# Merge stage of a hybrid encoder layer: weights loaded raw and parted on the spot, and no longer parted ahead by GpSimd

## The chip, the cores and the metric

One core of a Trainium2 chip runs the whole layer in one launch. The metric is the device time of the launch in microseconds (us). An engine takes its instructions strictly in the order in which they stand in its queue: PE (TensorE), DVE (VectorE), ACT (ScalarE), POOL (GpSimd) and SP (SyncE, which here only issues transfers). A wait at the head of a queue holds everything behind it.

## The reference

`x` is 1024 positions by 1024 channels. The layer is

```
h      = LayerNorm(x) * (1 + sc1) + sh1            # sh, sc, g: from c through w_ada
q,k,v, f, q,k,v, gate_a, gate_c = split(h @ w_in)
o_a    = forgetting attention, 8 heads             # causal, bias from a cumulated gate
o_c    = chunk attention, 8 heads                  # 64-position chunks, own and 8 before, learned bias
merged = sigmoid(gate_a) * (o_a @ w_br_fox) + sigmoid(gate_c) * (o_c @ w_br_chunk)
x      = LayerNorm(alpha * x + (1 + g1) * (merged @ w_out))
h      = LayerNorm(x) * (1 + sc2) + sh2
x      = LayerNorm(alpha * x + (1 + g2) * (convolved, gated MLP of h))
```

All is float32. A product of two float32 matrices is made of three PE products: each operand is **parted** into a rounded high part and the rest, `hi = round(x)`, `lo = x - hi`, and `hi*hi + hi*lo + lo*hi` is summed.

## The kernel before, in words

The work goes through stages: the first norm and modulation, attention with the projections beside it, the merge stage, the up-projection, the down-projection. A scheduler places the instructions on each engine's queue; the code gives it the program order.

**Attention.** `plan` goes through pairs of heads, the eight chunk heads first (pairs 4 to 7), then the eight forgetting heads. Scores are made by PE (L442, L443), a bias is added and the extreme taken by DVE (L451), the exponential by ACT (L457), PE turns the result (L494), ACT and DVE part it (L497, L498), and PE multiplies by v (L508). A chunk head's bias tile `cb` comes from DRAM, but two 64x64 corners of it are the mask, and these are written by POOL: `load_bias`, L415 and L416. There are eight such pairs of memsets, one for each chunk head, and the first L451 of a head reads its tile. The tile has two buffers; the call for a head comes when the head before it starts.

**Side work.** While attention runs, the generator `side_work` feeds POOL. It is advanced by the attention loop (`next(beside, None)`) and yields twice for each job, so jobs and memsets stand on the POOL queue in the order in which the loop came by. A job is one of three kinds:

- split job, 16 of them: load a 512 KB weight tile of `w_out` or `w_br` (L546), round it (L550, two halves), take the rest (L553, two halves), store both (L595, two stores of 512 KB) into the DRAM tensors `wod` and `brd`;
- combining job, 19 of them: load two weight tiles, make four sums or differences of halves (L588, four instructions), store two tiles into `wd` (8 jobs, from `w_up`) or `td` (11 jobs, from `w_down`);
- vector job, 32 of them: load a tile of `w_ada`, two products with the conditioning (L556) and two sums into `acc` (L559).

They are dealt in groups of seven, "jajaaja": three jobs (j) and four vector jobs (a). The j list holds the 16 split jobs first, then the 8 of `w_up`, then the 11 of `w_down`. Tiles `dr` have four buffers in turn, so a load waits for the stores of the tile four places before it. After the side work POOL loads and scales the first attention outputs (L788, L792, L793).

**Merge stage.** For each half of the positions, `merge` multiplies by the branch weights (eight sets `c`, 24 matmuls each, `psb`) and gates (`sg`, loaded by SP; L928, L934 to L938), and `mix` multiplies by `w_out` (eight sets `k`, 24 matmuls each, `psm`). In the first half both go set by set. In the second half `merge(1)` has the norms of the first half beside it (`norms`: DVE, ACT, and stores `xd` on POOL, L994), two of the `w_out` sets are fetched early into a pool of their own (`widened`, `wide`), and `mix(1)` does set 0 for all four position tiles, then each tile with all the other sets.

A set is fetched by `parted_w` (L907 to L913): two loads of 512 KB from `wod` or `brd` on SP, straight into `wh`, `wl`, or, for every third set, into the two buffers of `ws`. No engine touches it before PE.

Of the kernel before, what the change touches and what calls it, by code (L numbers as in the profile page):

```python
# [12 lines left out]
F32 = mybir.dt.float32  # L13
F32R = mybir.dt.float32r
# [5 lines left out]
P = 128  # L20
S = 1024
D = 1024
NT = S // P
KD = D // P
H = 512
# [19 lines left out]
def body(ctx, tc, a, out):  # L45
# [50 lines left out]
    wod = dram.tile([KD, 4, P, H], F32, name="wod", tag="wod")  # L96
    brd = dram.tile([KD, 4, P, H], F32, name="brd", tag="brd")

    def load_w(src, shape):
        if shape[-1] == P:  # L100
# [414 lines left out]
    def side_work():  # L515
# [1 line left out]


        sub = ALU.subtract
        jobs = [([src.rearrange("p (j n) -> p j n", j=2), None], None, dst)  # L520
                for srcs, dst in ((a["w_out"], wod), (a["w_br"].rearrange("c p k n -> c p (k n)"), brd))
                for src, dst in zip([srcs[k] for k in range(KD)], [dst[k] for k in range(KD)])]
        ups = ((3, 2, 3, ALU.add), (2, 0, 2, sub), (0, 3, 0, sub), (1, 1, 0, sub))
        downs = ((0, 1, 0, sub), (1, 3, 1, sub), (3, 3, 0, sub), (2, 2, 3, sub))
        for c in range(HEAD):
# [16 lines left out]
        def fetch():  # L542
            while len(tiles) < min(len(loads), free[0]):
                x = ap.tile([P, 2, H], F32, name=nm("dr"), tag="dr", bufs=4)
                if loads[len(tiles)] is not None:
                    po.dma_start(out=x, in_=loads[len(tiles)])  # L546
                tiles.append(x)

        def copied(x, y, j):
            po.tensor_copy(out=y[:, j, :].bitcast(F32R), in_=x[:, j, :])  # L550

        def rest(x, y, j):
            po.tensor_sub(out=x[:, j, :].bitcast(F32R), in0=x[:, j, :], in1=y[:, j, :].bitcast(F32R))  # L553

        def product(acc, x, k):
            po.tensor_scalar_mul(x[:, k % 2, :] if k else acc, x[:, k % 2, :], cond[:, k : k + 1])  # L556
# [7 lines left out]
        for m, (srcs, what, dst) in enumerate(mixed):  # L564
            xs = tiles[at : at + len(srcs)]
            while bias:
                bias.pop()()
            if due and m >= due[0][0] + LAG:
                _, acc_, v, half = due.pop(0)
                ps = pmm.tile([P, H], F32, name=nm("psada"), tag="mm")  # L570
                ada_sums(ps, acc_, H)
                bias.append(partial(late_bias, ps, v, half))
            if dst is None:
                v, half, q = what
                if q == 0:
# [6 lines left out]
            elif what is None:  # L582
                ops = [partial(f, *xs, j) for f in (copied, rest) for j in range(2)]
            else:
                blocks = [x[:, j, :] for x in xs for j in range(2)]
                ops = [partial(po.tensor_tensor, out=blocks[o], in0=blocks[p], in1=blocks[q], op=op) for o, p, q, op in what]
            for j, op in enumerate(ops):
                op()  # L588
# [312 lines left out]

    if True:

        sets = count()

        def parted_w(src, pool=None):

            tags = ("wh", "wl") if pool or next(sets) % 3 < 2 else ("ws", "ws")
            parts = [(pool or wp).tile([P, 2, H], F32R, name=nm(g), tag=g) for g in tags]
            for x, j in zip(parts, (2, 0)):  # L910
                sy.dma_start(out=x.bitcast(F32), in_=src[j : j + 2].rearrange("j p n -> p j n"))
            return parts

        def merge(half, os_, beside, ahead=iter(())):
            ms = []
# [2 lines left out]
            def branch(c, b):  # L918
                if c not in held:
                    sg = mx.tile([P, 2, H], F32, name=nm("sgl"), tag="sgl", bufs=2)  # L920
                    sy.dma_start(out=sg, in_=gd[half, 2 * c : 2 * c + 2].rearrange("b p s -> p b s"))
                    held[c] = [x.rearrange("p j (k n) -> p (j k) n", k=4) for x in parted_w(brd[c])], sg
# [21 lines left out]
        def mix(half, ms, beside, wide=None, ended=None, rest=None):  # L944
# [5 lines left out]
            def add(t, k, w):  # L950
                mh, ml = ms[k]
                ts = slice(t * P, (t + 1) * P)
                for n in range(2):
                    pe.matmul(ps[t][n], mh[:, ts], w[0][:, n, :], start=k == 0, stop=False)
                    pe.matmul(ps[t][n], mh[:, ts], w[1][:, n, :], start=False, stop=False)
                    pe.matmul(ps[t][n], ml[:, ts], w[0][:, n, :], start=False, stop=k == end)

            end = 3 if wide else KD - 1
            late = []
            for k in range(1 if wide else KD):  # L960
                w = parted_w(wod[k])
                for t in range(4):
                    add(t, k, w)
                next(beside, None)
            if wide:
                late += [(k, parted_w(wod[k])) for k in (1, 2)]
                late += sorted(wide.items()) + [(k, parted_w(wod[k], rest)) for k in (6, 7)]
            xs = []
            for t in range(4):
                tt = 4 * half + t  # L970
                xx = mx.tile([P, D], F32, name=nm("xr"), tag="xr", bufs=4)
                sy.dma_start(out=xx, in_=a["x"][tt * P : (tt + 1) * P, :])
                xs.append(xx)
# [70 lines left out]
        reading = load_o(1, o1, (4, 6, 2, 0), mx, "xr", 4, mx, "xr")  # L1044
        xs0 = mix(0, m0, chain((None,) * 2, reading))
        x0, x1 = [], []
        wide_cm, widep = opened(name="wide", bufs=2)
        wide = {}

        def widened():  # L1050
            sy.dma_start(out=l1g, in_=a["ln1_g"].partition_broadcast(P))
            sy.dma_start(out=l1b, in_=a["ln1_b"].partition_broadcast(P))
            for _ in range(5):
                yield
            for k in (4, 5):
                wide[k] = parted_w(wod[k], widep)
                yield

        beside = norms(0, xs0, x0)
# [400 lines left out]
```

## Time and profile before

| what | us |
|---|---|
| runs of the kernel before | 1547.07, 1549.76, 1550.41; median 1549.76 |
| span of the profiled execution | 1548.2 |
| PE busy in it | 1502.7 |
| POOL busy in it | 658.2 |
| attention with its projections, about | 95 to 697 |
| first attention output loaded by POOL after the side work | 651.06 |
| `merge(1)`, first to last matmul | 794.7 to 847.7 |

The profile is that of one execution. Its span runs from the first to the last instruction; the median of the runs is 1.6 us above it, which is what lies around the span and between executions. A row of a timeline has the start, the duration, the engine, the line of the kernel and what is written from what; in square brackets stands how long the engine sat idle ahead of it and whom it waited for. A row of groups has the busy time, the mean in nanoseconds, and the idle time before. In a table of stretches each engine has its busy time, then follow PE's granted clock and the share of time in which the DMA engines were busy.

### The profile page before, as it was taken

How to read it: one execution, taken by the hardware profiler on the slowest of the kernel's cores; microseconds unless marked ns; L12 is line 12 of the kernel's file. 1: busy time of each engine (PE TensorE's matmuls, PEld its weight loads, DVE VectorE, ACT ScalarE, POOL GpSimd, SP SyncE). 2: the span in 40 equal slices, each digit the busy share in tenths (PEclk: the TensorE clock that was granted, in tenths of full speed). 3: DMA queues.
4: the chain of work that ended last, by engine and by line, in shares of the span. 5: the costliest groups of instructions: out<-in, count | busy, mean ns of one | idle time of the engine just before them, and what ended most of it. 6: DMA issues, size and time to landing. Idle time of an engine off the chain costs nothing.

```text
span 1548.2 us, 21760 instructions
## 1 busy us (share of the span) xinstructions
PE 1502.7 (97%) x7663; PEld 1264.7 (82%) x7663; DVE 1034.5 (67%) x2038; ACT 709.5 (46%) x1316; POOL 658.2 (43%) x607
## 2 busy tenths in 40 slices
PE   6999999999999999999998999999999999999996
PEld 3788898889889888888886877888888888888885
DVE  6756566566656565554468587777778776845798
ACT  3545555554544454442112165544544554555451
POOL 0039897787878776730000005454455443000000
PEclk9999999999999999999999999999999999999998
DMA  9156666756576578758999575443344322697552
GB/s 366 50 165 215 217 192 198 218 194 216 189 233 220 189 260 299 260 151 292 308 323 347 214 258 190 140 154 132 122 140 147 115 102 104 246 328 255 191 190 75
DMA packets 129756, 317.54 MB, mean 205 GB/s; under 512 B 13024, under 2 KB 21936, under 8 KB 129648
## 3 DMA queue, kind: packets, MB, share of 16 engines
q1 hardware_dynamic: 90208, 197.83, 37.8%
q0 software_dynamic: 25344, 92.02, 17.8%
q10 hardware_dynamic: 14096, 26.31, 4.8%
q8 instruction: 60, 0.98, 0.3%
q14 instruction: 48, 0.39, 0.1%
HBM read 223.47 MB, written 84.25 MB: 199 GB/s over the span
## 4 chain that ended last, share of the span: by engine, by line
PE 72%; POOL 9%; DMA 8%; DVE 7%; issue 2%; ACT 1%; SPq 0%; ACTq 0%; DVEq 0%; POOLq 0%
PE psu L859 25%; PE psd L1277 4%; PE psd L1278 4%; PE psd L1276 4%; PE pso L508 3%; DMA wod<-dr 3%; PE psg L192 3%; PE psg L194 3%; PE psg L193 3%; POOL dr L553 2%; PE pst L494 2%; POOL acc L559 2%; POOL dr L556 2%; PE psq L194 2%; DMA brd<-dr 2%
## 5 line engine op out<-in xcount | busy, mean ns | idle before, releaser
L859 PE MATMUL psu<-hc,wx 128*128 128x512 f32 x792 | 185.7, 389 | 0.1
L859 PEld LDWEIGHTS psu<-hc,wx 128*128 128x128 f32 x792 | 148.6, 188 | 31.3 <-ACT u L1202 0.5
L1125 DVE SCALAR_TENSOR_TENSOR pcv<-u,convp,pcv 128x1024 f32<-128x1024 f32 x88 | 113.1, 1286 | 45.4 <-ACT pcv L1123 44.4
L1266 DVE TENSOR_TENSOR op<-rw,op 128x512 fp32r<-128x512 f32 x146 | 93.4, 687 | 52.8 <-ACT op L1265 52.5
L1265 ACT CAST op<-rw 128x512 fp32r<-128x512 f32 x146 | 85.2, 622 | 85.4 <-PE psd L1278 39.8
L457 ACT ACTIVATE s<-s,mx 128x640 f32<-128x640 f32 (+7 forms) x128 | 94.5, 738 | 58.6 <-DVE mx L451 57.4
L1277 PE MATMUL psd<-op,op 128*128 128x512 f32 x292 | 113.6, 389 | 0.9 <-DVE op L1266 0.9
L1278 PE MATMUL psd<-op,op 128*128 128x512 f32 x292 | 113.6, 389 | 0.0
L1276 PE MATMUL psd<-op,op 128*128 128x512 f32 x292 | 113.1, 389 | 0.0
L497 ACT CAST pt<-pst 128x512 fp32r<-128x512 f32 (+1 forms) x192 | 82.1, 450 | 62.3 <-PE pst L494 60.8
L498 DVE TENSOR_TENSOR pt<-pst,pt 128x512 fp32r<-128x512 f32 (+1 forms) x192 | 96.0, 519 | 17.2 <-ACT pt L497 15.5
L192 PE MATMUL psq<-h1h,wh 128*128 128x512 f32 x256 | 103.8, 407 | 1.7 <-DVE h1h L188 1.3
L192 PE MATMUL psg<-h1h,wh 128*128 128x512 f32 x256 | 103.7, 405 | 0.0
L194 PE MATMUL psq<-h1h,wl 128*128 128x512 f32 x256 | 100.9, 394 | 0.9 <-DVE wl L112 0.9
L194 PE MATMUL psg<-h1h,wl 128*128 128x512 f32 x256 | 100.3, 392 | 0.5 <-DVE wl L112 0.5
L193 PE MATMUL psq<-h1l,wh 128*128 128x512 f32 x256 | 100.8, 394 | 0.0
L193 PE MATMUL psg<-h1l,wh 128*128 128x512 f32 x256 | 100.2, 391 | 0.0
L556 POOL TENSOR_SCALAR dr<-dr,cond 128x512 f32<-128x512 f32 x56 | 89.9, 1607 | 8.1 <-DMA dr<-in_w_ada 7.1
L508 PE MATMUL pso<-pt,vs 128*128 128x256 f32 x608 | 90.4, 288 | 1.3 <-DVE pt L498 1.2
L994 POOL DMA_DIRECT2D xd<-xr x8 | 4.4, 545 | 199.3 <-DVE xr L992 199.3
L508 PEld LDWEIGHTS pso<-pt,vs 128*128 128x128 f32 x608 | 81.1, 191 | 8.7 <-DVE pt L498 2.6
L112 DVE TENSOR_TENSOR wl<-ws,wh 128x1024 fp32r<-128x1024 f32 x38 | 61.2, 1611 | 39.1 <-ACT wh L111 39.1
(286 smaller groups left out, 4001.3 us busy)
## 6 DMA issues: line engine op xcount, KB each, us to landing
ws<-in_w_up SPq DMA_DIRECT2D x34, 512.0 KB, 3.7
dr<-in_w_ada POOLq DMA_DIRECT2D x32, 512.0 KB, 4.8
dr<-in_w_down POOLq DMA_DIRECT2D x22, 512.0 KB, 4.8
td<-dr POOLq DMA_DIRECT2D x22, 512.0 KB, 4.7
rw<-td SPq DMA_DIRECT2D x44, 256.0 KB, 4.5
yd<-y SPq DMA_DIRECT2D x20, 512.0 KB, 2.7
rw<-yd SPq DMA_DIRECT2D x40, 256.0 KB, 4.2
rw<-sd SPq DMA_DIRECT2D x33, 256.0 KB, 4.6
```

Of the source, the lines that this page charges most:

```text
L192: pe.matmul(ps, wh, xh, start=start, stop=False)
L193: pe.matmul(ps, wh, xl, start=False, stop=False)
L194: pe.matmul(ps, wl, xh, start=False, stop=stop)
L457: se.activation(out=st[:, 0:nk], in_=st[:, 0:nk], func=AF.Exp, scale=-1.0, bias=prev, accum_out=sums[:, col : col + 1])
L498: ve.tensor_sub(out=dl, in0=src, in1=dh)
L508: pe.matmul(ps[:, 0:256], vs[:, h % 2, j0 + j, :], pt[j // 4][:, c, j % 4, :], start=j == 0 and c == 0, stop=j == nj - 1 and c == 1)
L556: po.tensor_scalar_mul(x[:, k % 2, :] if k else acc, x[:, k % 2, :], cond[:, k : k + 1])
L859: pe.matmul(ps, w[:, a_, k, :], h[k][b_], start=first, stop=k == 3 and a_ == 1, skip_group_check=on)
L1125: ve.scalar_tensor_tensor(out=ps, in0=u[b][:, 2 - d : S + 2 - d], scalar=cp[:, 2 - d : 3 - d], in1=ps, op0=ALU.mult, op1=ALU.add)
L1276: pe.matmul(ps[t], g[:, 0, ts], d[:, 0], start=start, stop=False, skip_group_check=on)
L1277: pe.matmul(ps[t], g[:, 0, ts], d[:, 1], start=False, stop=False, skip_group_check=on)
L1278: pe.matmul(ps[t], g[:, 1, ts], d[:, 0], start=False, stop=stop, skip_group_check=on)
```

## The change

The split jobs, `wod` and `brd` go. `side_work` starts with the combining jobs. `parted_w` loads a raw 512 KB tile into `ws` (two buffers), lets ACT round it into `wh` (two buffers) and POOL subtract into `wl` (two buffers). The early pool `wide` holds three sets (3, 4, 5) in place of two, and `mix(1)` fetches set 3 there and no longer last.

```
-        jobs = [([src.rearrange("p (j n) -> p j n", j=2), None], None, dst)
-                for srcs, dst in ((a["w_out"], wod), (a["w_br"].rearrange("c p k n -> c p (k n)"), brd))
-                for src, dst in zip([srcs[k] for k in range(KD)], [dst[k] for k in range(KD)])]
+        jobs = []
...
-        sets = count()
-
         def parted_w(src, pool=None):
-
-            tags = ("wh", "wl") if pool or next(sets) % 3 < 2 else ("ws", "ws")
-            parts = [(pool or wp).tile([P, 2, H], F32R, name=nm(g), tag=g) for g in tags]
-            for x, j in zip(parts, (2, 0)):
-                sy.dma_start(out=x.bitcast(F32), in_=src[j : j + 2].rearrange("j p n -> p j n"))
-            return parts
+            st = wp.tile([P, D], F32, name=nm("ws"), tag="ws")
+            sy.dma_start(out=st, in_=src)
+            hi, lo = [(pool or wp).tile([P, 2, H], F32R, name=nm(g), tag=g) for g in ("wh", "wl")]
+            st = st.rearrange("p (j n) -> p j n", j=2)
+            se.copy(out=hi, in_=st)
+            po.tensor_sub(out=lo, in0=st, in1=hi)
+            return hi, lo
...
             if wide:
-                late += [(k, parted_w(wod[k])) for k in (1, 2)]
-                late += sorted(wide.items()) + [(k, parted_w(wod[k], rest)) for k in (6, 7)]
+                late += [(k, parted_w(a["w_out"][k])) for k in (1, 2)] + sorted(wide.items())
+                late += [(k, parted_w(a["w_out"][k], rest)) for k in (6, 7)]
...
-            if wide:
-                late.append((3, parted_w(wod[3])))
...
-        wide_cm, widep = opened(name="wide", bufs=2)
+        wide_cm, widep = opened(name="wide", bufs=3)
...
-            for _ in range(5):
+            for _ in range(4):
                 yield
-            for k in (4, 5):
-                wide[k] = parted_w(wod[k], widep)
+            for k in (3, 4, 5):
+                wide[k] = parted_w(a["w_out"][k], widep)
                 yield
```

In the rows below an instruction's line is that of its own kernel: the changed kernel's L541, L545, L548, L575, L582, L413 are L546, L556, L559, L588, L595, L415 of the kernel before.

The POOL queue just ahead of the mask of the last chunk head, before:

```order
L595 DMA brd<-dr_3661 128x2x512
L595 DMA brd<-dr_3563 128x2x512
L556 TENSOR_SCALAR dr_3662<-dr_3662,cond 128x512
L546 DMA dr_3712<-in_w_ada 128x2x512
L546 DMA dr_3787<-in_w_br 128x1024
L556 TENSOR_SCALAR dr_3662<-dr_3662,cond 128x512
L556 TENSOR_SCALAR dr_3712<-dr_3712,cond 128x512 x2
L415 MEMSET cb_3463 64x64
```

and after:

```order
L575 TENSOR_TENSOR dr_3574<-dr_3574 128x512
L541 DMA dr_3674<-in_w_ada 128x2x512
L575 TENSOR_TENSOR dr_3574<-dr_3672,dr_3574 128x512
L575 TENSOR_TENSOR dr_3672<-dr_3672,dr_3574 128x512
L582 DMA td<-dr_3574 128x2x512
L575 TENSOR_TENSOR dr_3672<-dr_3672 128x512
L545 TENSOR_SCALAR dr_3674<-dr_3674,cond 128x512
L582 DMA td<-dr_3672 128x2x512
L541 DMA dr_3724<-in_w_ada 128x2x512
L545 TENSOR_SCALAR dr_3674<-dr_3674,cond 128x512
L541 DMA dr_3799<-in_w_down 128x1024
L413 MEMSET cb_3474 64x64
```

Counted over the whole queue, what stands ahead of the masks of the last four chunk heads was 7, 10, 12 and 14 split jobs with 8, 12, 15 and 18.5 vector jobs; it is now 6.25, 8.25, 11.25 and 14.25 combining jobs with 7.5, 10.5, 14.5 and 17.5 vector jobs. The masks stand after nearly as many jobs, but after jobs of another kind.

The POOL queue in `merge(1)`, where there were only the four stores `xd` of the norms, is now (`wl` from `ws` and `wh`: the rest of a set; the sets are branch 3, branch 4, `w_out` 3, branch 5, `w_out` 4, branch 6, `w_out` 5, branch 7):

```order
L897 TENSOR_TENSOR wl_8602<-ws_8599,wh_8601 128x1024
L977 DMA xd<-xr_8389 128x1024
L897 TENSOR_TENSOR wl_8662<-ws_8659,wh_8661 128x1024
L897 TENSOR_TENSOR wl_8701<-ws_8698,wh_8700 128x1024
L977 DMA xd<-xr_8391 128x1024
L897 TENSOR_TENSOR wl_8730<-ws_8727,wh_8729 128x1024
L897 TENSOR_TENSOR wl_8769<-ws_8766,wh_8768 128x1024
L977 DMA xd<-xr_8393 128x1024
L897 TENSOR_TENSOR wl_8797<-ws_8794,wh_8796 128x1024
L897 TENSOR_TENSOR wl_8836<-ws_8833,wh_8835 128x1024
L897 TENSOR_TENSOR wl_8864<-ws_8861,wh_8863 128x1024
```

So from branch 5 on, branch sets and early `w_out` sets take turns in the two `ws` buffers. Each raw load on SP stands in the same turn, and waits for the POOL subtraction two sets before it.

More of the change, by code (lines that the diff above doesn't have):

```diff
@@ L95, in body @@
     rowd = dram.tile([2, D], F32, name="rowd", tag="rowd")
-    wod = dram.tile([KD, 4, P, H], F32, name="wod", tag="wod")
-    brd = dram.tile([KD, 4, P, H], F32, name="brd", tag="brd")
     def load_w(src, shape):
@@ L544, in fetch @@
                 x = ap.tile([P, 2, H], F32, name=nm("dr"), tag="dr", bufs=4)
-                if loads[len(tiles)] is not None:
-                    po.dma_start(out=x, in_=loads[len(tiles)])
+                po.dma_start(out=x, in_=loads[len(tiles)])
                 tiles.append(x)
[L549 to L553, printed above, removed]
         def product(acc, x, k):
@@ L581, in side_work @@
                     due.append((m, acc, v, half))
-            elif what is None:
-                ops = [partial(f, *xs, j) for f in (copied, rest) for j in range(2)]
             else:
@@ L921, in branch @@
                     sy.dma_start(out=sg, in_=gd[half, 2 * c : 2 * c + 2].rearrange("b p s -> p b s"))
-                    held[c] = [x.rearrange("p j (k n) -> p (j k) n", k=4) for x in parted_w(brd[c])], sg
+                    held[c] = [x.rearrange("p j (k n) -> p (j k) n", k=4) for x in parted_w(a["w_br"][c].rearrange("p k n -> p (k n)"))], sg
                 (bh, bl), sg = held[c]
@@ L955, in add @@
                     pe.matmul(ps[t][n], mh[:, ts], w[1][:, n, :], start=False, stop=False)
-                    pe.matmul(ps[t][n], ml[:, ts], w[0][:, n, :], start=False, stop=k == end)
-            end = 3 if wide else KD - 1
+                    pe.matmul(ps[t][n], ml[:, ts], w[0][:, n, :], start=False, stop=k == KD - 1)
             late = []
             for k in range(1 if wide else KD):
-                w = parted_w(wod[k])
+                w = parted_w(a["w_out"][k])
                 for t in range(4):
```

## The prediction

> **What bounds the kernel now.** First the page's span and engine rows, then the table of stretches, then the chain of waits and the timelines around its turning points.
>
> ```profile
> span 1548.2 us, 21760 instructions
> PE 1502.7 (97%) x7663; PEld 1264.7 (82%) x7663; DVE 1034.5 (67%) x2038; ACT 709.5 (46%) x1316; POOL 658.2 (43%) x607
> ```
>
> PE is busy for all but 45 us: a change off PE can win only part of those, and can lose without limit by making PE wait. Stretches (PE, PEld, DVE, ACT, POOL, granted clock, DMA share, GB/s):
>
> ```profile
> 300.00:350.00 50.00, 48.33 (x301) 43.25 (x300) 30.99 (x84) 26.89 (x62) 43.64 (x44) 1.00 0.60 200
> 800.00:820.00 20.00, 19.91 (x88) 16.16 (x87) 19.40 (x43) 3.94 (x7) 1.15 (x2) 1.00 0.82 296
> 820.00:840.00 20.00, 14.83 (x64) 11.33 (x62) 18.05 (x45) 3.94 (x8) 1.07 (x2) 0.98 0.99 370
> 840.00:860.00 20.00, 19.57 (x75) 15.91 (x75) 7.42 (x24) 6.97 (x9) 1.08 (x2) 0.85 0.89 319
> ```
>
> In the attention (300 to 350) POOL is the busiest engine beside PE, 43.64 of 50 us before its transfers and waits are counted. In the merge stage (800 to 860) POOL has nothing to do, the DMA engines are full, and PE loses some microseconds. The chain of waits shows where POOL sets PE's time:
>
> ```profile
> 327.74 3.11 POOL dr L556 x2
> 330.85 0.10 POOL cb L415
> 330.97 0.04 DVE s L451
> 333.09 0.76 PE pst L494 x5
> ```
>
> A product of a vector job (L556), then the mask of a chunk head (L415), then the scores on DVE, then a transpose on PE that came late. So the last mask already ends on the critical path. Masks on POOL, and the moments at which DVE used or wanted them:
>
> ```profile
> 250.92 0.16 POOL L415 MEMSET cb<- 64x64 f32 x1
> 291.71 0.17 POOL L415 MEMSET cb<- 64x64 f32 x1
> 330.79 0.14 POOL L415 MEMSET cb<- 64x64 f32 x1
> ```
> ```profile
> 260.45 0.23 DVE L451 CUSTOM_DVE_ANT_0 s<-pss,cb 128x128 f32<-128x128 f32 x1
> 294.62 0.29 DVE L451 CUSTOM_DVE_ANT_0 s<-pss,cb 128x128 f32<-128x128 f32 x1
> 327.65 0.55 DVE L486 MEMSET pt<- 128x256 f32 x2
> 330.97 0.29 DVE L451 CUSTOM_DVE_ANT_0 s<-pss,cb 128x128 f32<-128x128 f32 x1 [2.77 <-POOL cb L415]
> ```
>
> The sixth mask was written 9.5 us ahead of its use (250.92, 260.45), the seventh 2.9 us (291.71, 294.62), the eighth after DVE was free for it at 328.2 (327.65 + 0.55): DVE waited 2.77 us. POOL falls behind during the chunk heads and has no slack left at their end.
>
> **The change, part by part.** *POOL beside the attention.* Fewer jobs, but the 16 light ones went, and they stood first; the heavy ones move ahead of the masks. The price of both kinds in place, waits included:
>
> ```profile
> 98.86 1.17 POOL L550 CAST dr<-dr 128x512 fp32r<-128x512 f32 x2 [2.86 <-issue]
> 303.38 0.73 POOL L550 CAST dr<-dr 128x512 fp32r<-128x512 f32 x1
> 369.88 1.30 POOL L588 TENSOR_TENSOR dr<-dr 128x512 f32<-128x512 f32 x1 [2.09 <-DMA dr<-in_w_up]
> 491.67 1.52 POOL L588 TENSOR_TENSOR dr<-dr 128x512 f32<-128x512 f32 x1 [2.11 <-DMA dr<-in_w_up]
> ```
> ```profile
> L556 POOL TENSOR_SCALAR dr<-dr,cond 128x512 f32<-128x512 f32 x56 | 89.9, 1607 | 8.1 <-DMA dr<-in_w_ada 7.1
> L559 POOL TENSOR_TENSOR acc<-acc,dr 128x512 f32<-128x512 f32 x56 | 75.3, 1345 | 1.7
> L546 POOL DMA_DIRECT2D dr<-in_w_ada x31 | 23.8, 766 | 33.6 <-DMA brd<-dr 13.4 <-DMA wod<-dr 12.2 <-DMA wd<-dr 6.7
> ```
>
> From the first rounding of split job 1 to that of job 13 there are four groups of three split and four vector jobs: (303.38 - 98.86) / 4 = 51.1 us a group. From the first sum of the first `w_up` job to that of the seventh there are two groups of three combining and four vector jobs: (491.67 - 369.88) / 2 = 60.9 us. A vector job takes 2 x 1.607 + 2 x 1.345 + 0.766 = 6.7 us. So a split job costs (51.1 - 26.8) / 3 = 8.1 us and a combining job (60.9 - 26.8) / 3 = 11.4 us: four sums in place of two roundings and two subtractions, two loads in place of one, and the same stores.
>
> Ahead of the eighth mask were 14 split and 18.5 vector jobs: 113 + 124 = 237 us, where the trace has 330.8 - 98.9 = 231.9; I scale by 231.9 / 237 = 0.978. Now it is 14.25 combining and 17.5 vector jobs: 162 + 117 = 280 us, scaled 273: the mask is written at 372, **41.3 us later**. The seventh: 11.25 x 11.4 + 14.5 x 6.7 = 225, scaled 220, at 319, due at 294.6: 24 late. The sixth: 8.25 and 10.5 jobs, 161 us, at 260, just in time. So PE waits twice, at the seventh mask for about 23 us and, everything having moved by that, at the eighth for about 18 more. Behind the waiting DVE instruction stand the parting of probabilities and of weights, so ACT and PE have little else to do; PE's chain ran through the last mask already. Since the eighth mask was on the chain before, its delay counts in full: +41.3. Bounds: if the combining jobs ran at the split jobs' 8.1 us, the new count would be 233 us, scaled 228, 4 earlier than now; if POOL slowed as it does where its rows meet loaded DMA, 5% more on 273 is +14. I take 41.3, since the 60.9 us group is the same mix of jobs on the same queue.
>
> After the chunk heads no mask is left. The forgetting heads' bias is loaded by ACT's queue. POOL's whole list is then 19 x 11.4 + 32 x 6.7 = 431 us long, scaled 422, and ends near 520 (98.9 + 422), with the vector sums due only after the attention. PE is idle for 45 us in the whole span, so I count nothing won by that.
>
> *Clock.* A wait costs more than itself; the rows of the merge stage show it.
>
> ```profile
> 794.71 0.39 PE L192 MATMUL psb<-oh,wh 128*128 128x512 f32 x1
> 806.01 0.39 PE L192 MATMUL psb<-oh,wh 128*128 128x512 f32 x1
> 816.89 0.39 PE L192 MATMUL psb<-oh,ws 128*128 128x512 f32 x1
> 840.43 0.80 PE L194 MATMUL psb<-oh,ws 128*128 128x512 f32 x1 [1.42 <-DMA ws<-brd]
> 846.08 0.40 PE L194 MATMUL psb<-oh,ws 128*128 128x512 f32 x1
> 847.67 0.39 PE L954 MATMUL psm<-wh,mh 128*128 128x512 f32 x1
> ```
> ```profile
> PE psb L192 <- DVE st L119: 2.5, 1, 2.5
> PE psb L194 <- DMA wl<-brd: 1.7, 1, 1.7
> PE psb L194 <- DMA ws<-brd: 1.4, 1, 1.4
> ```
>
> From 840.43 to 846.08 thirteen matmuls went by in 5.65 us. At full clock 48 take 816.89 - 806.01 = 10.88, or 0.227 each, so 2.7 us went to the low clock after 2.5 and 1.4 us of waiting. After the seventh mask such a loss is swallowed by the eighth, whose time POOL sets; after the eighth it adds **2.7**. The Trainium skill ("TensorE: Matmul & The Clock Gate", "Why this matters for your kernels" and Part 1) says that gaps over about 3 us bring the half clock until about 3.4 us of work; by it the loss would be an estimated 1.7 us and the sum one lower. The low clock here came after shorter gaps that lay close together.
>
> *Merge stage.* `merge(1)` ran from 794.71 to 847.67, 53.0 us for 192 matmuls that need 43.5: 9.5 lost, to the three waits above and the low clock. Two of them are for parts from DRAM. The third is put down to DVE, but DVE was not short of time there (below); I count it as a transfer too. What takes the place of these waits:
>
> ```profile
> L880 ACT CAST hw<-sgl 128x1024 fp32r<-128x1024 f32 x2 | 2.1, 1053 | 10.1 <-DMA sgl<-in_w_up 10.1
> L793 POOL TENSOR_TENSOR ost<-ost,ort 128x1024 f32<-128x1024 f32 x3 | 7.8, 2601 | 17.7 <-DMA ost<-od 12.5 <-DMA ort<-rd 5.2
> ```
> ```profile
> ws<-in_w_up SPq DMA_DIRECT2D x34, 512.0 KB, 3.7
> wl<-brd SPq DMA_DIRECT2D x11, 512.0 KB, 6.2
> ```
>
> A set is now loaded once (512 KB, not 1 MB), rounded by ACT (1.05) and subtracted by POOL (2.6 by a product of the same size). A set of PE work is 24 x 0.227 = 5.44 us, so 3.65 us fit and leave 1.8. ACT and POOL had this room. But there are two raw buffers. From branch 5 on branch and early sets alternate, so three branch sets in a row each wait for the subtraction of the last: load 3.7 + 3.65 = 7.35 against 5.44, three times 1.9 less the 1.8 in hand: 3.9 us of waiting. With the 6.2 us that a load takes now it would be 3 x 4.4 - 1.8 = 11.4. I take 5, near the first, as the traffic of weights halves. In `mix(1)` set 2 goes into set 0's buffer: 3.65 after its release, with 6 x 0.227 = 1.36 of set 1 to cover it, 2.3 lost; set 7 follows set 2 through the raw buffer, 3.65 + 3.7 + 3.65 = 11.0 against six sets at 1.36 and the 2.3, another 0.5. Together 7.8 where `merge(1)` lost 9.5, and an estimated 0.6 on top for `mix(1)`, 10.1 in all: **-2.3**, with bounds of -10 (no wait at all) and +4, and more if a low clock follows. Set 3 moved early is in this sum. The `xd` stores ahead of three subtractions wait for DVE's norms, which came at least one set before; ACT's square roots likewise: nothing.
>
> ```profile
> L112 DVE TENSOR_TENSOR wl<-ws,wh 128x1024 fp32r<-128x1024 f32 x38 | 61.2, 1611 | 39.1 <-ACT wh L111 39.1
> L797 DVE TENSOR_TENSOR ol<-ost,oh 128x1024 fp32r<-128x1024 f32 x8 | 9.6, 1224 | 6.8 <-ACT oh L796 6.8
> ```
>
> Beside a busy POOL a DVE subtraction of this size took 1.61 us, alone 1.22. In `merge(1)` 24 such two-input instructions (L934, L938, L991, L992) would take up to 24 x 0.39 = 9 us more; DVE idled 60 - 19.40 - 18.05 - 7.42 = 15 us from 800 to 860, so I put this at nothing, at most +4. The Trainium skill ("SBUF — State Buffer", "Who interferes with whom") calls the shared port an exclusive lock: a two-input DVE instruction waits out a whole GpSimd one. By it the worst would be an estimated 2.6 us each, which speaks against this change; the trace has 0.39 us.
>
> *The sum.* The profile's span is 1548.2 and the median 1549.8, so differences go to the median: 1549.8 + 41.3 + 2.7 - 2.3 = 1591.5.
>
> **The rivals.** *The masks stay on time and the merge is freed.* In total POOL loses 16 x 8.1 = 130 us of work; if combining jobs early ran at 8.1 us, nothing would wait: -1.7 at the mask, -10.1 in the merge, 1538. Against it: the 60.9 us groups were measured in the same stage, at a DMA share no higher. 0.07. With the masks on time and the merge losing as much as before, no change: 0.04.
>
> *Half the lag.* With PE and DVE standing, transfers meet less traffic, and combining jobs cost 9.8, midway: 257 us, scaled 251, +19: 1570. For it: POOL's idle time ahead of loads is waiting for stores. 0.12.
>
> *The merge starves too.* Loads stay at 6.2 us, so 11.4 and not 5, and two low-clock spells of 2.7 and some waits in the first half follow: +13, 1605. 0.13.
>
> The forecast itself, masks late by 34 to 48 us: 0.64.
>
> **How the numbers follow.** A median of three runs spread over 3.3 us can tell 0.2%, 3 us, from no change. Slower by more: 0.64 + 0.12 + 0.13 = 0.89; within: 0.04; faster: 0.07. The range takes in the halved lag and the starved merge, 1568 to 1606; outside it lie the cases without a lag and a little on either side.
>
> **What would show it.** Right: the wait of DVE's L451 line for POOL grows from 2.8 us to about 42, at the seventh and eighth chunk heads; the eighth mask lies near 372; PE's idle time between 290 and 375 is about 40 us, with granted clocks under 1 behind it; POOL's side work ends near 520; the DMA share in the merge well under 0.9 and waits there for `wl` from POOL. Wrong: the eighth mask before 345, or PE waiting on something else there; or a merge stage more than 10 us longer or shorter than it was.

## The result, and the profile after

The changed kernel took 1597.12 us (median of five runs, 1595.42 to 1603.5) where the kernel before took 1547.07 beside it: a ratio of 1.0321 (95% interval 1.0303 to 1.0339), 50 us slower. The forecast was 1591.5.

First the page of the changed kernel, its span and engine rows: POOL has less work than before (641.8 us and not 658.2), and PE has 11 us more busy time and 37 us more idle time.

```profile
span 1596.5 us, 21672 instructions
PE 1513.7 (95%) x7663; PEld 1270.3 (80%) x7663; DVE 1057.7 (66%) x2038; ACT 739.8 (46%) x1348; POOL 641.8 (40%) x527
```

The masks of the last three chunk heads on POOL, and the scores on DVE that need the last two (start, duration, in brackets the idle time ahead and whom it waited for):

```profile
250.93 0.17 POOL L413 MEMSET cb<- 64x64 f32 x1
305.27 0.14 POOL L413 MEMSET cb<- 64x64 f32 x1
356.62 0.17 POOL L413 MEMSET cb<- 64x64 f32 x1
```
```profile
305.44 0.29 DVE L449 CUSTOM_DVE_ANT_0 s<-pss,cb 128x128 f32<-128x128 f32 x1 [10.63 <-POOL cb L413]
356.83 0.29 DVE L449 CUSTOM_DVE_ANT_0 s<-pss,cb 128x128 f32<-128x128 f32 x1 [17.45 <-POOL cb L413]
```

The sixth mask is as early as it was; the seventh and the eighth are 13.6 and 25.8 us later than before, and DVE stood still for 10.63 and 17.45 us where it had waited 2.77. PE then ran at a lower granted clock, as the stretches show (PE, PEld, DVE, ACT, POOL, clock, DMA share, GB/s); the last two rows are the merge stage:

```profile
300.00:350.00 50.00, 35.08 (x186) 30.35 (x186) 20.72 (x53) 18.58 (x42) 41.04 (x40) 0.85 0.57 187
350.00:400.00 50.00, 40.71 (x310) 39.22 (x311) 26.39 (x78) 20.81 (x57) 42.15 (x41) 0.88 0.60 186
850.00:900.00 50.00, 39.22 (x150) 29.96 (x149) 49.11 (x88) 17.79 (x27) 25.05 (x15) 0.90 0.60 210
900.00:950.00 50.00, 47.29 (x222) 38.46 (x221) 38.48 (x72) 19.53 (x31) 9.02 (x7) 1.00 0.50 185
```

A third wait was in no forecast. It is in the chain of waits, at the end of the side work: the last sum of the last vector on POOL, then PE's column sums of it (`psada`, L161; L163 before), with the rest of PE's queue behind them.

```profile
512.63 1.27 POOL acc L548
513.90 0.04 issue
513.95 1.87 PE psada L161 x8
```

How late PE is against the kernel before, matmul by matmul, gives the ledger. Each row is the start of the same matmul in both traces.

| matmul | before | after | late by |
|---|---|---|---|
| first transposes behind the eighth mask | 333.09 | 358.95 | 25.9 |
| scores a little later (low clock paid) | 342.75 | 370.63 | 27.9 |
| scores just ahead of the last column sums | 477.44 | 507.28 | 29.8 |
| projection a little behind them | 480.40 | 519.91 | 39.5 |
| `merge(0)` starts | 707.67 | 742.58 | 34.9 |
| `mix(0)` starts | 751.19 | 786.10 | 34.9 |
| `merge(1)` starts | 794.71 | 833.36 | 38.7 |
| `mix(1)` starts | 847.67 | 890.41 | 42.7 |
| up-projection starts | 895.55 | 943.92 | 48.4 |
| last matmul | 1535.89 | 1584.23 | 48.3 |

So the masks cost 28 us, the column sums 10, and 4.6 came back before the attention ended (no wait found here accounts for the 1.9 us between 27.9 and 29.8); the merge stage cost 13.5, spread over its last three parts: 3.8 in `mix(0)`, 4.0 in `merge(1)`, 5.7 in `mix(1)`.

In `merge(1)` the timelines of POOL, DVE and PE around one wait of PE show how. POOL:

```profile
852.40 0.60 POOL L977 DMA_DIRECT2D xd<-xr  x1 [3.54 <-DVE xr L975]
853.03 4.77 POOL L897 TENSOR_TENSOR wl<-ws,wh 128x1024 fp32r<-128x1024 f32 x2
862.54 0.58 POOL L977 DMA_DIRECT2D xd<-xr  x1 [4.75 <-DVE xr L975]
863.14 4.67 POOL L897 TENSOR_TENSOR wl<-ws,wh 128x1024 fp32r<-128x1024 f32 x2
```

DVE and PE (the norm's L974 and L975 are L991 and L992 before):

```profile
853.32 5.56 DVE L974 SCALAR_TENSOR_TENSOR xr<-xr,mv,l1g 128x1024 f32<-128x1024 f32 x1
860.86 1.27 DVE L975 SCALAR_TENSOR_TENSOR xr<-xr,r,l1b 128x1024 f32<-128x1024 f32 x1
863.46 5.45 DVE L974 SCALAR_TENSOR_TENSOR xr<-xr,mv,l1g 128x1024 f32<-128x1024 f32 x1
```
```profile
865.54 0.79 PE L192 MATMUL psb<-oh,wl 128*128 128x512 f32 x1 [3.54 <-POOL wl L897]
```

L974 begins just after POOL has begun two subtractions in a row. They end at 857.80 (853.03 + 4.77), L974 at 858.88, some 1.1 us later, about the time that it needs alone. It didn't run slower: it stood still until POOL was done. Behind it L975 is late, so the store `xd` at the head of POOL's queue waits for it (4.75 us), so the next subtraction begins at 863.14, although its operand was rounded before, so PE waits 3.54 us for `wl` and then runs its matmuls at a low clock (0.55 granted from 865.5 to 871). POOL's next pair meets the next L974. It is a ring: POOL holds DVE, and DVE's lateness holds POOL.

ACT's queue closes the same ring a second time. The rounding of a raw tile stands there behind a cast that waits for DVE (L923, the high part of the merged result):

```profile
870.99 0.62 ACT L923 CAST mh<-sgl 128x512 fp32r<-128x512 f32 x1 [6.88 <-DVE sgl L920]
871.52 2.00 ACT L896 CAST wh<-ws 128x1024 fp32r<-128x1024 f32 x2
```

And since a raw load waits for the subtraction that frees its buffer, the loads of the last branch sets were issued at 855.47, 865.52 and 875.55, ten microseconds apart, where a set is 5.44 us of PE work.

### The profile page after: what moved, and what is told of

It reads as the page before. It is cut to its first block, busy times and chain, and to the rows that moved or that the text cites. A ratio compares the mean times of both kernels' runs of the same rounds, so it can differ in the third digit from the quotient of the medians.

```text
span 1596.5 us, 21672 instructions
## 1 busy us (share of the span) xinstructions
PE 1513.7 (95%) x7663; PEld 1270.3 (80%) x7663; DVE 1057.7 (66%) x2038; ACT 739.8 (46%) x1348; POOL 641.8 (40%) x527
## 4 chain that ended last, share of the span: by engine, by line
PE 59%; POOL 16%; DMA 10%; DVE 9%; issue 4%; ACT 2%; SPq 0%; DVEq 0%; POOLq 0%; ACTq 0%
PE psu L846 25%; POOL dr L575 5%; POOL acc L548 4%; POOL dr L545 4%; PE psd L1260 4%; PE psd L1261 4%; PE psd L1259 4%; DMA td<-dr 3%; PE psg L190 2%; PE psg L192 2%; PE psg L191 2%; PE pso L506 2%; POOL dr L541 2%; PE pst L492 1%; DMA dr<-in_w_down 1%
## 5 line engine op out<-in xcount | busy, mean ns | idle before, releaser
L897 POOL TENSOR_TENSOR wl<-ws,wh 128x1024 fp32r<-128x1024 f32 x32 | 77.9, 2440 | 126.7 <-ACT wh L896 124.4
L492 PE MATMUL pst<-ident,s 128*128 128x128 f32 x528 | 84.4, 276 | 25.8 <-DVE pt L496 25.7
L545 POOL TENSOR_SCALAR dr<-dr,cond 128x512 f32<-128x512 f32 x56 | 92.1, 1647 | 5.7 <-DMA dr<-in_w_ada 4.9
L492 PEld LDWEIGHTS pst<-ident,s 128*128 128x128 f32 x528 | 63.5, 142 | 32.6 <-DVE pt L496 26.1
```

Source lines behind the costliest of these rows:

```text
L492: pe.transpose(ps[:, b * P : (b + 1) * P], st[:, c0 : c0 + P], ident)
```

## The experiments

Each ratio is against runs of the kernel before on the same chip, whose medians were 1547.07 to 1551.88 us. Stage times are from the first matmul of a stage to that of the next, in the profiled execution; "late" is the start of `merge(0)` against 707.67.

| run | us | ratio (95%) | late | merge(0) | mix(0) | merge(1) | mix(1) |
|---|---|---|---|---|---|---|---|
| before | 1547.07 | | 0 | 43.5 | 43.5 | 53.0 | 47.9 |
| changed | 1597.12 | 1.0321 (1.0303 to 1.0339) | 34.9 | 43.5 | 47.3 | 57.0 | 53.5 |
| attn_only | 1580.92 | 1.0188 (1.0153 to 1.0222) | 33.8 | 43.5 | 43.6 | 51.8 | 48.0 |
| merge_only | 1563.87 | 1.0087 (1.0062 to 1.0112) | -0.3 | 43.5 | 47.8 | 55.5 | 55.0 |
| masks_dve | 1600.44 | 1.0320 (1.0292 to 1.0347) | 35.7 | 43.5 | 47.3 | 55.5 | 55.8 |
| masks_dve_sums_late | 1578.60 | 1.0185 (1.0156 to 1.0214) | 9.9 | 43.7 | 50.5 | 55.4 | 56.5 |
| heavy_first | 1577.14 | 1.0167 (1.0144 to 1.0189) | 27.5 | 43.5 | 43.5 | 51.0 | 49.2 |
| paced | 1571.25 | 1.0149 (1.0121 to 1.0176) | 5.5 | 43.5 | 47.3 | 57.1 | 52.9 |
| xd_on_act | 1599.93 | 1.0340 (1.0309 to 1.0370) | 43.7 | 43.5 | 47.5 | 55.3 | 53.5 |
| three_raw | 1606.37 | 1.0373 (1.0347 to 1.0399) | 42.9 | 47.5 | 44.3 | 55.9 | 54.2 |
| sub_on_dve | 1600.31 | 1.0336 (1.0305 to 1.0367) | 36.7 | 43.5 | 46.7 | 64.3 | 48.3 |
| memset_for_sub | 1583.73 | 1.0231 (1.0204 to 1.0258) | 31.0 | 43.5 | 43.5 | 43.5 | 53.7 |
| copy_for_sub | 1587.76 | 1.0249 (1.0217 to 1.0282) | 40.8 | 43.5 | 43.5 | 47.9 | 53.3 |
| paced_norms_pool | 1582.47 | 1.0223 (1.0197 to 1.0249) | 5.2 | 43.5 | 47.3 | 74.5 | 49.5 |

The column "late" is that of one execution each: kernels with the same attention lie between 31 and 44, so the merge stage is read from its own columns.

### Each part alone

The attention part: the kernel before, with

```
-        jobs = [(... w_out -> wod, w_br -> brd ...)]
+        jobs = []
...
-                late += [(k, parted_w(wod[k])) ...
+                late += [(k, parted_w(wd[k])) ...        # brd -> td likewise
```

> The kernel before with only the attention part of the change: no split jobs; the merge stage fetches its ready-made parts as before, but from wd and td (same shapes and transfers, other numbers), so the output is not the layer's. If the two parts of the change add up as the ledger of PE's start times says (merge(0) starts 34.9 us late, 13.4 more come after), this takes 1547 + 35 = 1582 us. If the merge stage's loss is a consequence of the late attention (or the other way round), it takes 1597 or close to 1547.

The merge part: the changed kernel with the `side_work` of the kernel before.

> The changed kernel with the old side work, split jobs included; nobody reads what they store. If the parts add up: 1547 + 13 = 1560 us, with PE waiting for wl from POOL in merge(1) and mix(1) as in the changed kernel. By the prediction's sum for the merge stage (-2.3) it would take 1545. If the loss there needs the late attention, 1547.

Measured: 33.8 us late ahead of an unchanged merge stage, and no lateness ahead of one that is 13.9 us longer. The ratios, 1.88% and 0.87%, sum to 2.75% where both together gave 3.21%. The starts of the stages add up (33.8 + 13.9 = 47.7 us where the changed kernel has 48.4); the ratios do so only at the edge of their intervals. Each part has its loss without the other, so neither causes the other. The forecast's -2.3 us for the merge stage is refuted here.

### Why the attention is late

Theory "backlog": POOL's list runs at its own pace, and whatever PE needs from it first pays. Theory "masks": the two late masks are the cost.

```
-            po.memset(b[0:DH, 576:640], NEG)
-            po.memset(b[DH:P, 0:64], NEG)
+            ve.memset(b[0:DH, 576:640], NEG)
+            ve.memset(b[DH:P, 0:64], NEG)
```

> The changed kernel with the 16 mask memsets on DVE, ahead of the scores that need them on the same queue. Theory 'masks': DVE's two waits for POOL (10.6 and 17.5 us) were the cost, so some 28 us go: 1569 us. Theory 'backlog': POOL's list is no shorter, its last vector sum still ends near 514 us, and PE, which would reach the last two column sums near 478 to 486, waits there for 28 to 32 us: only 2 to 6 us go, 1591 to 1595 us.

No gain at all. The masks are gone from POOL's queue, and PE's waits for the column sums of the last two vectors have grown from 5.95 us to these, as its timeline shows:

```profile
494.35 1.87 PE L161 MATMUL psada<-ones,acc 128*128 128x1 f32 x8 [3.75 <-POOL acc L548]
513.95 1.87 PE L161 MATMUL psada<-ones,acc 128*128 128x1 f32 x8 [16.67 <-POOL acc L548]
```

The second stands at 513.95 in both kernels. That it agrees to the hundredth is chance: in the other runs with the changed kernel's attention it came between 509.18 and 521.52. But POOL's list did not end earlier for PE's having been spared the masks. PE was 12.4 us late before those two (the matmul of 378.70 came at 391.10), and DVE had a hand in that:

```profile
164.56 5.37 DVE L110 TENSOR_TENSOR wl<-ws,wh 128x1024 fp32r<-128x1024 f32 x1 [2.12 <-ACT wh L109]
```
```profile
163.53 1.58 POOL L545 TENSOR_SCALAR dr<-dr,cond 128x512 f32<-128x512 f32 x1
165.07 1.29 POOL L575 TENSOR_TENSOR dr<-dr 128x512 f32<-128x512 f32 x1
166.31 1.28 POOL L548 TENSOR_TENSOR acc<-acc,dr 128x512 f32<-128x512 f32 x1
167.56 1.28 POOL L575 TENSOR_TENSOR dr<-dr,dr 128x512 f32<-128x512 f32 x1
168.79 0.60 POOL L541 DMA_DIRECT2D dr<-in_w_up  x1
```

DVE's subtraction began inside a product of POOL's and ended at 169.93, 1.1 us after POOL's last sum in that row of four and beside the issue of a load. That is the hold of `merge(1)` again, here over four POOL instructions. In this run the 34 L110 of the attention took 1.95 us on average, in the changed kernel 1.55.

Then the tail of the side work was moved as well:

```
+        for _ in range(200):
+            yield
         for _, acc_, v, half in due:
```

> As the run with the masks on DVE, and the column sums of the last two vectors are written behind the attention loop and not right behind the last job. Theory 'backlog': both joins with POOL are now gone but for the sixth sum (POOL ready at 453, PE there at 448), so the attention loses 0 to 6 us: 1597 - 29 to 1597 - 35, 1562 to 1568 us; the 13 us of the merge stage stay. Theory 'masks': the same time as with the masks alone.

With both joins moved the lateness fell from 35.7 to 9.9 us, so the backlog explains most of it. It was 11 to 17 us slower than I expected. Part of the 9.9 are holds like the one above (a wait of PE of 3.69 us at 260.13 for DVE); and the merge stage took 206.1 us and not 201.3; the reason is open.

The reverse, from the kernel before: the same jobs, and only their order changed.

```
-        jobs = [(... w_out -> wod, w_br -> brd ...)]
+        light = [(... w_out -> wod, w_br -> brd ...)]
+        jobs = []
...
+        jobs += light
```

> The kernel before with its list of side jobs reordered and nothing else: the 19 combining jobs first, the 16 split jobs behind them. The same work on POOL, the merge stage untouched, 658 us of POOL busy as before. Theory 'backlog': the masks of the seventh and eighth chunk heads come as late as in the changed kernel, DVE waits for them some 28 us in all; behind the last vector job more jobs follow, so the last column sums come six jobs later and the 9 us there go: merge(0) starts 25 to 30 us late, 1573 to 1578 us. If what hurt was that the split jobs are missing (a shorter list, an earlier end), nothing changes: 1548.

The masks come where they come in the changed kernel, to 2 us, with POOL's work untouched; its page and its DVE waits:

```profile
PE 1505.3 (96%) x7663; PEld 1266.5 (80%) x7663; DVE 1032.9 (66%) x2038; ACT 709.1 (45%) x1316; POOL 659.1 (42%) x607
```
```profile
307.12 0.14 POOL L415 MEMSET cb<- 64x64 f32 x1
...
358.25 0.17 POOL L415 MEMSET cb<- 64x64 f32 x1
```
```profile
DVE s L451 <- POOL cb L415: 27.8, 2, 17.0
```

27.8 us of waiting, `merge(0)` 27.5 us late, 1577.14 us. So the waits for the masks, the larger part of what the change does to the attention, come from the order of the list alone: this list is as long as that of the kernel before. The column sums are another matter. Here eleven split jobs follow the last vector job and PE waits for no column sum; in the changed kernel nothing follows, and there the shorter list does count.

And the remedy within the changed kernel, two more turns of the loop for each combining job:

```
+            if dst is not None:
+                yield
+                yield
             at += len(srcs)
```

> The changed kernel in which the side work pauses two more turns of the attention loop after each combining job, so that fewer jobs stand ahead of each mask (11.25 combining and 12 vector jobs ahead of the eighth, and not 14.25 and 17.5) and the list is dealt out over a longer stretch. Theory 'backlog': masks and column sums are on time, all 35 us of the attention go and the 13.5 of the merge stage stay: 1561 us (1558 to 1565). If fewer or later jobs don't help since DVE and POOL hold each other up beside the attention anyway, some 5 to 10 us more.

Its waits of DVE for the masks:

```profile
DVE s L449 <- POOL cb L413: 3.3, 1, 3.3
```

PE waits for no column sum, `merge(0)` starts 5.5 us late and not 34.9; the merge stage's loss stays, 200.8 us for its four parts as in the changed kernel. At 1571.25 us it is slower than I expected by 6 to 13, and still slower than the kernel before.

### Why the merge stage is slower

Three theories: the raw buffers (the prediction's), the order on POOL's queue (subtractions behind `xd`), and the hold. The first two edits:

```
-                po.dma_start(out=xd[4 * half + t], in_=xx)
+                se.dma_start(out=xd[4 * half + t], in_=xx)
```

> The changed kernel with the norms' stores xd issued by ACT's queue and not by POOL's. Theory 'order': in merge(1) POOL's next subtraction stands behind an xd store that waits for DVE's xr; without that the waits of 3.5, 2.0 and 1.7 us for wl go with their low clock, 1597 - 7 to 1597 - 10. Theory 'raw buffers' (the prediction's): the loop load, rounding, subtraction stays, 1597 to 1595. Theory 'lock' (DVE's instructions with two SBUF inputs stand still while POOL subtracts): L974 still takes over 3 us on average; PE gains some of the 7 us.

```
-            st = wp.tile([P, D], F32, name=nm("ws"), tag="ws")
+            st = mx.tile([P, D], F32, name=nm("wr"), tag="wr", bufs=3)
```

> The changed kernel with three raw buffers of their own in the merge stage in place of the two ws. Theory 'raw buffers' (the prediction's): the loop no longer binds, 5 to 8 us go: 1589 to 1592. Theories 'order' and 'lock': the raw tile is there in time already, wl is late for another reason: 1595 to 1599.

Neither helps `merge(1)` much. With `xd` elsewhere PE's waits for `wl` there are 2.0, 1.7 and 1.9 us in place of 3.5, 2.0 and 1.7, but one of 1.6 for the rounding is new, and the stage takes 55.3 us and not 57.0. The ring goes on by way of ACT, as one turn of it shows: POOL holds L974 and then L920, ACT's cast waits for L920, and the rounding stands behind the cast, at 870.19.

```profile
860.14 3.70 POOL L897 TENSOR_TENSOR wl<-ws,wh 128x1024 fp32r<-128x1024 f32 x1 [2.31 <-ACT wh L896]
863.81 3.37 POOL L897 TENSOR_TENSOR wl<-ws,wh 128x1024 fp32r<-128x1024 f32 x1
```
```profile
862.23 2.70 DVE L974 SCALAR_TENSOR_TENSOR xr<-xr,mv,l1g 128x1024 f32<-128x1024 f32 x1
864.85 2.88 DVE L920 TENSOR_TENSOR sgl<-sgl 128x512 f32<-128x512 f32 x1
```
```profile
867.76 0.62 ACT L923 CAST mh<-sgl 128x512 fp32r<-128x512 f32 x1 [4.24 <-DVE sgl L920]
```

The raw buffers are in this turn too: the branch loads were issued at 863.87, 873.94 and 883.24, each within 0.05 us of the end of the subtraction that freed its buffer. The group of L974 in that stage:

```profile
L974 DVE SCALAR_TENSOR_TENSOR xr<-xr,mv,l1g 128x1024 f32<-128x1024 f32 x4 | 8.6, 2160 | 0.0
```

I had expected over 3 us; it fell to 2.16, and other instructions with two operands were held in its place (L920, 0.68 us in the kernel before, took 1.37). With three raw buffers `merge(1)` takes 55.9 and `mix(1)` 54.2, so there the raw buffers alone are not what binds; in `mix(0)`, which falls from 47.3 to 44.3, they were most of the loss. No run has both edits, so what three buffers would give with `xd` on ACT's queue is not shown. (`merge(0)` is 4 us longer there because the new buffers, in a pool that opens with the stage, are loaded later: PE waits 5.6 us for the first rounding.)

The subtraction on DVE:

```
-            po.tensor_sub(out=lo, in0=st, in1=hi)
+            ve.tensor_sub(out=lo, in0=st, in1=hi)
```

> The changed kernel with the subtractions of the merge stage's weights on DVE and not on POOL. Theory 'lock': DVE gets 32 instructions of 1.2 us but its own are no longer held: in merge(1) L974 falls from 4.2 us to 1.3; mix(0), merge(1) and mix(1) lose 3 to 8 us and not 13.5: 1585 to 1592. Theory 'raw buffers' (the prediction's): the loop gets 1.2 us shorter a set, 1597 - 4. Were DVE simply too full (49 of 50 us busy from 850 to 900), it would be slower: 1600 or more.

`mix(1)` falls to 48.3 us, what it took before, and L974 to 1.28 us, as the hold would have it; but `merge(1)` takes 64.3, for DVE had no room there: 13.3 us of subtractions came on top of an engine that was already full (49.11 of 50 us busy from 850 to 900 in the changed kernel), and they stand behind the norms.

```profile
L897 DVE TENSOR_TENSOR wl<-ws,wh 128x1024 fp32r<-128x1024 f32 x11 | 13.3, 1207 | 0.0
```

Two runs show the hold with another instruction of the same size in POOL's place:

```
-            po.tensor_sub(out=lo, in0=st, in1=hi)
+            po.memset(lo.bitcast(F32), 0.0)          # memset_for_sub
+            po.tensor_copy(out=lo, in_=st)           # copy_for_sub
```

> The changed kernel with POOL's subtraction in the merge stage replaced by a memset of wl to zero: the low parts of those weights are left out. POOL writes as many bytes and stands in the same place behind the same xd stores, but reads nothing. Theory 'lock': L974 and L975 take 1.3 us again, PE's waits for wl go, 1597 - 8 to 1597 - 13. Theory 'order' alone: the waits behind xd stay as far as xr is late, gain below 4 us. Theory 'raw buffers': the loop loses POOL's 2.4 us, 1597 - 5.

> The changed kernel with POOL's subtraction in the merge stage replaced by a copy of the raw tile into wl (the low parts of those weights are wrong). Against the run with the memset it differs in one thing: POOL reads SBUF while it writes, and no more than the memset does it wait for ACT's rounding. Theory 'lock': DVE's instructions with two SBUF inputs are held again; L974 takes over 2 us on average and merge(1) takes 48 to 56 us and not 43.5. If it was the missing wait for ACT's rounding that freed the merge stage, L974 takes 1.3 us and merge(1) 43.5 to 45.

With the memset, which reads nothing, three of the four parts take 43.5 us, no wait left at all. The groups of DVE and POOL in `merge(1)`, memset first, then copy:

```profile
L974 DVE SCALAR_TENSOR_TENSOR xr<-xr,mv,l1g 128x1024 f32<-128x1024 f32 x4 | 5.1, 1271 | 0.0
```
```profile
L897 POOL MEMSET wl<- 128x1024 f32 x8 | 7.7, 957 | 25.3 <-PE psb L192 20.9 <-PE psm L941 4.5
```
```profile
L974 DVE SCALAR_TENSOR_TENSOR xr<-xr,mv,l1g 128x1024 f32<-128x1024 f32 x4 | 7.2, 1790 | 0.0
```
```profile
L897 POOL CAST wl<-ws 128x1024 fp32r<-128x1024 f32 x11 | 11.9, 1085 | 29.0 <-DMA ws<-in_w_br 15.6 <-PE psb L192 9.0 <-PE psm L941 4.4
```

The memsets hold nothing: an L975 that began at 853.56, inside the memset of 853.19 to 854.15, took 1.28 us. The copy takes hardly longer than the memset (1.08 and 0.96 us) and waits as little for ACT, but it reads. Under it L974 is held again, twice in four: 2.13 and 2.50 us beside 1.27 and 1.26. So the POOL instruction that reads SBUF can hold DVE, and the one that only writes did not.

The stage times do not isolate the hold as well. `merge(1)` takes 47.9 us with the copy, just under the 48 to 56 I gave, and the mean of 1.79 is under the 2 us. But the copy, unlike the memset, also waits for the raw tile and keeps its buffer, and PE's one wait in that stage is for a rounding that waited for a raw load (issued at 867.64, when the copy before had freed the buffer):

```profile
876.19 0.69 PE L190 MATMUL psb<-oh,wh 128*128 128x512 f32 x1 [2.44 <-ACT wh L896]
875.09 1.04 ACT L896 CAST wh<-ws 128x1024 fp32r<-128x1024 f32 x1 [3.27 <-DMA ws<-in_w_br]
```

So the 4.4 us between copy and memset are not shown to be the hold: the loop through the raw buffers, the prediction's, is in them. How the other 9 us of `merge(1)` divide between the subtraction's length, which sets how long it holds DVE, and the wait for ACT's rounding, which both runs drop, they leave open too. `mix(1)` stays at 53 to 54 us in both: PE waits there for DVE (3.0 and 2.5 us, 2.67 in the changed kernel) and for ACT's rounding of `w_out` set 2 (1.8 and 1.5).

Last, the attempt to keep DVE out of POOL's way: the first half's norms with their scale on ACT, gain and bias on POOL.

```
-                ve.scalar_tensor_tensor(out=xx, in0=xx, scalar=mv[:, 0:1], in1=l1g, ...)
-                ve.scalar_tensor_tensor(out=xx, in0=xx, scalar=r, in1=l1b, ...)
+                se.activation(out=xx, in_=xx, func=AF.Identity, scale=r, bias=b)
+                po.tensor_tensor(out=xx, in0=xx, in1=l1g, op=ALU.mult)
+                po.tensor_tensor(out=xx, in0=xx, in1=l1b, op=ALU.add)
```

> As the paced kernel, and the first half's norms scale on ACT and take their gain and bias on POOL (two instructions a tile), so that DVE has no 1024-wide instruction with two SBUF inputs left in merge(1) beside POOL's subtractions; POOL then has some 19 us more there, 40 of the stage's 53. Theory 'lock': merge(1) falls from 57 to 45 to 50 us, its queue on POOL being the limit; 1548 to 1555. If POOL becomes the bound: no gain, 1561 or more.

It fell through: `merge(1)` took 74.5 us. PE's waits there are for POOL, now the bound:

```profile
PE psb L192 <- POOL wl L900: 15.8, 4, 8.7
```

No version beats the kernel before.

## Why the prediction was right, and where it was not

The direction, the mechanism in the attention and the total were right: 41.7 us slower was forecast and 50 came. But the total fits by luck: wrong terms of opposite sign cancel. One of the signs of being wrong that the forecast named, a merge stage more than 10 us longer than it was, came true (13.5 us).

**The masks: right in kind, too large.** Forecast +41.3 and 2.7 for the clock; measured 25.9 and 2.0. The sixth mask on time, the seventh and eighth late, the eighth's delay counting in full (25.8 us on the mask, 25.9 on PE), the first low clock swallowed by the second wait: as forecast. But the two waits were forecast at about 23 and 18 us and DVE's were 10.63 and 17.45, and the eighth mask came at 356.6 and not 372. Mis-sized is the price of a combining job. From POOL's first sum at 100.61 to the mask at 356.62 are 256 us; less 17.5 vector jobs at 6.7 that leaves 139 for 14.25 combining jobs, 9.7 us each and not 11.4 x 0.978 = 11.1. That is almost the price of the rival "half the lag" (9.8). The 11.4 came from groups at 370 to 492 in the trace of before. Most of the difference is idle time of POOL, above all until a store freed a tile: 23.9 us for the six combining jobs there, 4.0 each, and 37.9 us for the 14.25 here, 2.7 each. Why it waited less isn't settled.

**The column sums: the step that failed.** "With the vector sums due only after the attention" was taken from where their result is used. PE multiplies each finished vector by ones as soon as the list has gone six jobs on, and the last two when the list ends; that instruction stands in the middle of PE's queue, with the projections behind it. In the kernel before, eleven combining jobs followed the last vector job; now vector jobs come last, so the sums of the last two vectors are asked for one behind the other, while POOL is still behind. Cost 9.7 us (29.8 to 39.5). The run with the masks on DVE shows that both are one bill: with the first join gone, PE waits 20.4 us at this one.

**"Nothing is won" after the masks**: 4.6 us came back between 520 and 708, when POOL had little left to do (0.00, 7.54 and 5.52 us busy in the three stretches of 50 us from 550 to 700). Beside it PE was busy 50.00 us in each of the three stretches from 550 to 700; in the kernel before it had 49.41, 49.93 and 48.80 in 500 to 650.

**The merge stage: wrong in sign.** Forecast -2.3, measured +13.5. The transfers behaved as forecast (the DMA share fell from 0.82 and more to 0.50 and 0.60), and in `mix(1)` the two waits for sets 2 and 7 were there, 1.24 and 1.46 where 2.3 and 0.5 were forecast; a third, 2.67 us for DVE at 895.97, was not in the sum. Nor had DVE 15 us to give where it was held: of the 15 that the forecast counted, 12.6 lay after 840, and from 800 to 840 it was busy 37.45 of 40 us. Two steps failed:

- The price of POOL beside DVE. I took 0.39 us for each two-input instruction from the means of two groups, 1.61 and 1.22. A mean hides it: of those 38 instructions 17 took 1.15 to 1.25 us and 21 took 1.41 to 3.13. L974 cost 4.16 us on average here and 1.27 before (the rows below: `merge(1)` of the changed kernel, then of the kernel before). The sentence from the Trainium skill that I set beside it ("SBUF — State Buffer", "Who interferes with whom": an exclusive lock, the loser is fully blocked) speaks for the larger price, the trace agrees with it, and I let the mean overrule it.
- "The `xd` stores ahead of three subtractions wait for DVE's norms, which came at least one set before": they came late, as DVE was held, and POOL's queue waited 3.54 and twice 4.75 us for them. ACT's part, put at nothing in the same place, failed in the same way: its rounding stood up to 6.88 us behind a cast that waited for DVE.

```profile
L974 DVE SCALAR_TENSOR_TENSOR xr<-xr,mv,l1g 128x1024 f32<-128x1024 f32 x4 | 16.6, 4160 | 0.0
```
```profile
L991 DVE SCALAR_TENSOR_TENSOR xr<-xr,mv,l1g 128x1024 f32<-128x1024 f32 x4 | 5.1, 1272 | 0.0
```

The rival "the merge starves too" had the size, +13 on the forecast, and the wrong cause: it had the loads stay at 6.2 us, and they took 3.8 to 4.0 in the median (`w_br`, `w_out`). Its loop through the two raw buffers was real, but three buffers alone gave 3.0 us in `mix(0)` and 1.1 in `merge(1)`.

## What to carry to other kernels

Work given to a spare engine costs less by its sum than by its order: what stands ahead of the things that others wait for, at each of the places where they wait. Taking the light jobs off the head of a list made the engine's total smaller and its deliveries later; go through every join of that queue, the small ones in the middle of another engine's queue too, and remember that removing the first late join only moves the wait to the next. And price an instruction that another engine can hold up by its longest instances beside that engine, not by a group's mean.

## What the runs showed of the hardware

DVE with two operands in SBUF can be held while a POOL instruction reads SBUF, and it can stand still for several of them in a row: 5.56 us over two subtractions, 5.37 us over a product and three sums, and each time it ended 1.1 us after POOL's last. It does not always wait for the whole row. With `xd` on ACT's queue an L974 got in between two subtractions (862.23 to 864.93, the first of them ending at 863.84), and the second then took 3.37 us where 2.4 is usual: DVE holds POOL too. What decides whose turn it is isn't shown. Small ones pay as well, and an instruction with an operand in PSUM does not, as these three in `merge(1)` of the changed kernel show:

```profile
846.16 2.70 POOL L897 TENSOR_TENSOR wl<-ws,wh 128x1024 fp32r<-128x1024 f32 x1 [3.83 <-ACT wh L896]
```
```profile
846.59 0.66 DVE L914 SCALAR_TENSOR_TENSOR sgl<-sgl,psb 128x512 f32<-128x512 f32 x1
847.18 1.70 DVE L127 SCALAR_TENSOR_TENSOR t<-y,v 128x1 f32<-128x1 f32 x1
```

L914 (one operand in PSUM) takes its 0.66 us in the middle of POOL's subtraction; L127, one element a partition and 0.21 us elsewhere, ends at 848.88, 0.02 us after POOL.
